# Feed-forward blocks: refilled forms, earlier weights, separate sums, and six orders of products

## The chip, the cores and the metric

The kernel runs on one core of one Trainium2 chip. The metric is the device time in microseconds (us). TensorE (PE in the profile) multiplies, VectorE (DVE) and ScalarE (ACT) work on tiles, GpSimd (POOL) does small jobs, and SyncE (SP) issues most of the DMAs, in the order of its queue. Weight loads of PE are listed as PEld.

## The reference

One layer of a decoder is computed for 1024 prompt tokens and 8 sample tokens, 1032 columns in all, in fp32:

```
x += W_merge( g_A*conv_branch + g_B*ssd_branch + g_C*mem_attn_branch )
x += SwiGLU(RMSNorm(x))          # D_MODEL 1024, FFN_HIDDEN 2816
final RMSNorm
swiglu(xn) = (silu(xn @ w_gate) * (xn @ w_up)) @ w_down
```

The mixers read one wide input projection `w_in` (12320 columns); the feed-forward part (FFN) has 22 blocks of 128 hidden rows (j = 0 to 21) each for gate and up, and then the down projection.

## The kernel before

Activations lie transposed, with 128 channels on the partitions and the 1032 tokens along the row. A product in fp32 is made from three: each operand is split into a high part `hi` (a copy rounded by ACT, `S.copy`) and a rest `lo` (`V.tensor_sub`, DVE), and PE adds hi·hi, hi·lo and lo·hi.

Most of the input projection and nearly all of the FFN go through `strassen` (L302). It takes two blocks of 128 output channels, splits weights and activations into quadrants (two halves of the contraction, two halves of 516 tokens), and needs 7 products instead of 8. `st_prod` (L254) is one product: 4 slices of the contraction (kt), 3 split terms, 2 parts of the columns (`HALF`: 256 and 260), 24 matmuls; a block has 7 products and 168 matmuls. Its order is: slice, term, part.

The seven sums of activations, the *forms* B11, T1, nT2, B21, T3, B22, T4, are made once for all blocks and kept as `hi` and `lo` tiles of the pool `ap_` (tags `ah` and `al`, 12 buffers each; T4 has a pool of its own). Two slices share one tile of 2 x 520 columns, of which 2 x 516 are used. The weights of a block come as `raw1` and `raw2` (pool `raw`, three buffers); `st_adds2` (L291) writes two sums of weights into `raw1` itself, and four `st_split` make the weight pairs A, S, T and D (three buffers for `hi`, three for `lo`). The three PSUM tiles m0, m1 and m2 change roles from block to block (L320): the tile of the last product (`pa`) is the tile of the next block's fourth (`pc`, B21).

In the FFN, `hidden_pair` runs `strassen` for gate and up of two blocks; then silu and the elementwise product (L1850 to L1852) follow on ACT and DVE. For j below 16 the forms of the product are written to DRAM (`hf_d`), for j from 16 on the product itself (`h_d`). The down projection (`d00` to `d06`, `d10` to `d16`, two halves of the contraction with four blocks each) is again `strassen`, adding into the residual rows x that are read back from DRAM (L1873). Its forms take the place of the old ones: `used(f)` is called when a block has finished with form f, and in the last block before a change (`u20` and `d06`) it calls `h_form` (L1833): two DMAs of 516 KB into tiles of the pool `ev` (5 buffers), then at once the split into the form's tiles (L389 on ACT, L390 on DVE). The last six hidden blocks go through the plain `gemm` (L204; 16 to 18) and a last stage (19 to 21).

The pool `ev` also holds the accumulators of the convolutions (`ax`, `sacc`), rows of the sampled states (`sr`), and one sum of weights (`sa`) of each FFN block.

The order of each engine's queue isn't the order of the text: Tile's planner places an instruction as soon as its inputs and its buffer are free by its own reckoning, the earlier text first. On the chip each queue then runs in that fixed order. So a load of the weights of `d00`, which stands after all of `h_form` in the text, is issued at 2203.0 us, ahead of most of the loads of the forms.

Of the kernel before, what the change touches and what calls it, by code (L numbers as in the profile page):

```python
# [17 lines left out]
P = 128  # L18
# [13 lines left out]
EPS = 1e-6  # L32
LAG = 3
GROUPS = 4
HEADS = 32
# [10 lines left out]
def tile_kernel(ctx: ExitStack, tc, a, o):  # L46
# [3 lines left out]
    def f32(t):  # L50
        return t.bitcast(F32)
# [25 lines left out]
    def pair_of(t):  # L77
        return t.rearrange("p (a c) -> p a c", a=2)[:, :, :HT]

    def act_pair(part, name):  # L80
        return pair_of(ap_.tile([P, AW], F32R, tag=part, name=name))

# [3 lines left out]
    def flat(ps):  # L86
        return banks(ps)[:, Z0 : Z0 + TT]
# [105 lines left out]

    def gemm(w, acts, name, width=P, off=0):

        hi, lo = w
        ps = mm_ps(name)
        nk = len(acts)
        n = int(pace[0] + pace[1])
        pace[1] += pace[0] - n  # L200
        marks = [nk * i // n for i in range(n)]
        between = seam.pop() if seam else None
        out = flat(ps)
        for k, (ah, al) in enumerate(acts):  # L204
# [6 lines left out]
            ks = slice(k * width + off, k * width + off + P)  # L211
            for i, (wt, x) in enumerate(((hi, ah), (hi, al), (lo, ah))):
                for c, n in FULL:
                    PE.matmul(  # L214
                        out[:, c : c + n], wt[:, ks], x[:, c : c + n],
                        start=(k == 0 and i == 0), stop=(k == nk - 1 and i == 2),
                    )
        return ps
# [6 lines left out]


    HS = [slice(0, HT), slice(HT, TT)]
    pst = [None]
# [3 lines left out]
    def hv(ps):  # L232
        return banks(ps)[:, Z0 : Z0 + HT]
# [20 lines left out]
    def st_prod(forms, ps, w, off, f, start):  # L254
        for kt in range(4):
            xh, xl = forms[f][kt]
            ks = slice(off + kt * P, off + (kt + 1) * P)
            for i, (wt, x) in enumerate(((w[0], xh), (w[0], xl), (w[1], xh))):
                for c, n in HALF:
                    PE.matmul(  # L260
                        hv(ps)[:, c : c + n], wt[:, ks], x[:, c : c + n],
                        start=(start and kt == 0 and i == 0), stop=(kt == 3 and i == 2),
                        skip_group_check=True,
                    )

# [24 lines left out]

    def st_adds2(raw1, raw2, sa):  # L291

        V.tensor_add(raw1[:, :512], raw1[:, :512], raw2[:, :512])
        V.scalar_tensor_tensor(
            raw1[:, 512:], sa[:, 512:], -1.0, raw1[:, 512:], op0=ALU.mult, op1=ALU.subtract
        )
        return raw1

    def st_sums2(raw1, raw2, sa, nm):
        return st_split(st_adds2(raw1, raw2, sa), f"{nm}T")  # L300

    def strassen(  # L302
        src1, src2, forms, nm, sums, outs, early=None, after_t3=None, ready=None, hook=None, into=False, refill=None
    ):
# [8 lines left out]
        def used(f):  # L313
            if refill is not None:
                refill(f)


        if ready is None and early is None:
            raw1, raw2 = st_raw(src1, f"{nm}r1"), st_raw(src2, f"{nm}r2")
# [8 lines left out]
        if early is None:  # L328
            pc = st_ps(tags[2], f"{nm}{tags[2]}")
            wA = st_split(raw1, f"{nm}A")  # L330
            prod(pa, wA, 0, "B11", True)
        else:
            tick()
# [11 lines left out]
        if ready is None:  # L345
            sb = st_adds2(raw1, raw2, sa)
        if early is None:
# [28 lines left out]
        tick()  # L376
        wD = st_split(raw2[:, 512:], f"{nm}D", 512)
        prod(pa, wD, 0, "T4", False)
# [1330 lines left out]
    forms = {}  # L1709
    fx = {}  # L1710

    def form(f, kt, src):
# [4 lines left out]
        split_to(*forms[f][kt], src)  # L1717

# [48 lines left out]
    pfx = st_stack.enter_context(tc.tile_pool(name="fx", bufs=2))  # L1767
    fx["T4"] = lambda part, nm: pair_of(pfx.tile([P, AW], F32R, tag=part, name=nm))

# [31 lines left out]
    g0 = (*g0, st_sums2(*g0[:3], "g0"))  # L1801
# [7 lines left out]
    def hidden_pair(nm, j, refill=None):  # L1809
# [12 lines left out]

        src = ffn[nm]
        pa = strassen(
            wblock(src, j * P), wblock(src, (j + 1) * P), forms, f"{nm}{j}",
            ev_sums, outs, e, ready=g0 if (nm, j) == ("g", 0) else None, refill=refill,
        )
        return o[0], o[1], pa if e is None else pa
# [4 lines left out]
    def h_form(ch, f):  # L1833

        for i in range(2):
            t = ev_tile(f"hf{ch}{f}{i}", (P, 2 * HT))
            SY.dma_start(t, hf_d[ch, FORMS.index(f), i])
            mk = fx.get(f) or act_pair
            hi, lo = mk("ah", f"h{ch}{f}{i}h"), mk("al", f"h{ch}{f}{i}l")
            split_to(hi, lo, t.rearrange("p (a c) -> p a c", a=2))  # L1840
            hforms[ch][f] += [(hi[:, a], lo[:, a]) for a in range(2)]

    hs = {}
    for j in range(0, NF, 2):
        s1, s2, pa = hidden_pair("g", j)
# [3 lines left out]
        u1, u2, pa = hidden_pair("u", j, (lambda f: h_form(0, f)) if j == NF - 2 else None)  # L1849
        V.tensor_mul(s1, s1, u1)  # L1850
        V.tensor_mul(s2[:, HS[1]], s2[:, HS[1]], u2[:, HS[1]])
        V.scalar_tensor_tensor(s2[:, HS[0]], pa, -1.0, s2[:, HS[0]], op0=ALU.mult, op1=ALU.mult)  # L1852
        if j >= 16:
            SY.dma_start(h_d[j - 16], s1)
            SY.dma_start(h_d[j - 15], s2)
# [10 lines left out]
    def w_rows(ch, m):  # L1866

        src = a["w_ffn_down"][0, ch * 1024 : (ch + 1) * 1024, m * P : (m + 1) * P]
        return src.rearrange("(k t p) c -> p t k c", t=2, p=P)

    for m in range(KD):
        x2[m] = big(f"x3_{m}")
        SY.dma_start(x2[m], x2_d[m])  # L1873
    for ch in range(2):
        for m in range(0, KD, 2):
            strassen(
                w_rows(ch, m), w_rows(ch, m + 1), hforms[ch], f"d{ch}{m}", ev_sums,
                lambda m=m: (x2[m][:, HS[0]], x2[m][:, HS[1]], x2[m + 1][:, HS[0]], x2[m + 1][:, HS[1]]),
                into=True, refill=(lambda f: h_form(1, f)) if ch == 0 and m == KD - 2 else None,
            )  # L1880
# [20 lines left out]
    def down(js, hs):  # L1901
        nk = len(js)
        for m in range(KD):
            nm = f"wd{js[0]}{m}"
            if nk * 256 <= 1024:
                if m % 2 == 0:
# [4 lines left out]
                    )  # L1911
                ps = gemm(w, hs, f"pd{js[0]}{m}", 256, (m % 2) * P)
            else:
# [101 lines left out]
```

## Time and profile before

| | |
|---|---|
| time, median of 3 runs | 2505.39 us (2504.51 to 2506.88) |
| the profiled execution: time, span | 2509.08 us, 2505.8 us |
| PE busy, matmuls | 2434.5 us (97%), 18906 |
| DVE, ACT, POOL busy | 1596.0, 1070.7, 116.3 us |
| mean granted clock of PE | 0.99 |
| an undisturbed block of `strassen` in the FFN, 168 matmuls | 19.93 us |
| gate and up blocks 6 to 20 | 1914.3 to 2233.1 us |
| down blocks | 2233 to 2411 us |

All times of instructions are us from the start of the span. A line "L260" is line 260 of the kernel before. In a timeline, the number in square brackets is how long the engine stood idle before the instruction, with what released it. PEclk is the granted clock of PE as a share of its full rate. The chain of waits goes from the last instruction back to what released each step.

### The profile page before, as it was taken

The numbers are of one execution on the slowest core, as the hardware profiler recorded it, in microseconds if no ns is written. First come the engines' busy times: TensorE is split into PE (matmuls) and PEld (weight loads), VectorE is DVE, ScalarE is ACT, GpSimd is POOL, SyncE is SP. The second block draws the span as 40 slices with busy tenths as digits, with TensorE's granted clock in tenths as the row PEclk, the third lists the DMA queues.
The fourth block names the chain that finished last, engine by engine and source line by source line (L and its number), as shares of the span: only waits on it lengthen the run. The fifth ranks groups of instructions, "written<-read, shape, count | busy, mean of one in ns | idle before, by whom it ended". The sixth has DMA issues, their size and how long they took to land.

```text
span 2505.8 us, 45588 instructions
## 1 busy us (share of the span) xinstructions
PE 2434.5 (97%) x18906; PEld 2315.8 (92%) x18906; DVE 1596.0 (64%) x2598; ACT 1070.7 (43%) x1716; POOL 116.3 (5%) x163
## 2 busy tenths in 40 slices
PE   7999999999999999999999989999999999999998
PEld 5899999999999999888888877899999999989998
DVE  5754586777677674656767562454777556566655
ACT  6554455354545435556544441223443333343222
POOL 0200010000000000221120000000000000000000
PEclk9999999999999999999999999999999999999999
DMA  6345434334344446567878677765444323274321
GB/s 197 106 128 167 131 107 145 114 117 127 124 127 128 134 150 209 171 214 253 265 230 283 202 262 237 263 235 158 149 158 127 110 89 111 68 268 141 100 85 68
DMA packets 356077, 404.80 MB, mean 162 GB/s; under 512 B 16422, under 2 KB 286870, under 8 KB 355863
## 3 DMA queue, kind: packets, MB, share of 16 engines
q1 hardware_dynamic: 335422, 344.18, 44.0%
q10 hardware_dynamic: 20449, 57.71, 5.9%
q8 instruction: 148, 2.42, 0.4%
q14 instruction: 58, 0.48, 0.1%
HBM read 286.74 MB, written 115.32 MB: 160 GB/s over the span
## 4 chain that ended last, share of the span: by engine, by line
PE 56%; DMA 4%; DVE 3%; ACT 1%; issue 1%; SPq 0%; ACTq 0%; DVEq 0%
PE po L214 12%; PE pm L1738 4%; PE ps_q L214 3%; PE pd L214 1%; PE py L981 1%; PE pss L994 1%; PE po L973 1%; PE d00m L260 1%; PE d10m L260 1%; PE Z14m L260 1%; PE G16m L260 1%; PE B6m L260 1%; PE C7m L260 1%; PE d16m L260 1%; PE d14m L260 1%; PE d02m L260 1%
## 5 line engine op out<-in xcount | busy, mean ns | idle before, releaser
L926 ACT ACTIVATE r<-r,acum 128x128 f32<-128x128 f32 x256 | 79.1, 391 | 3.8 <-DMA r<-ac_d 3.3
L867 ACT ACTIVATE st<-st,es 128x128 f32<-128x128 f32 x128 | 41.6, 394 | 61.4 <-DMA st<-in_state_ssm_dram 51.5
L697 DVE SCALAR_TENSOR_TENSOR ax<-u,prm,ax 128x1024 f32<-128x1024 f32 x44 | 56.3, 1280 | 0.0
L958 POOL TENSOR_TENSOR xdd<-xdt,decst 128x512 f32<-128x512 f32 x32 | 38.9, 1216 | 288.3 <-DVE xdt L954 288.3
L1385 DVE TENSOR_TENSOR yr<-po,yr 128x1032 f32<-128x1032 f32 x8 | 9.8, 1231 | 55.9 <-PE po L214 45.9
L977 DVE TENSOR_TENSOR y<-po,ea 128x512 f32<-128x512 f32 x28 | 19.3, 689 | 37.8 <-PE po L973 37.8
L952 DVE TENSOR_TENSOR r<-r,cbm 128x1024 f32<-128x1024 f32 x32 | 39.2, 1224 | 2.4
L869 DVE SCALAR_TENSOR_TENSOR st<-sr,dts,st 128x128 f32<-128x128 f32 x128 | 39.4, 345 | 0.4
L951 ACT COPY bT<-bp 128x128 f32<-128x128 f32 x32 | 8.5, 266 | 69.7 <-DVE cbm L949 69.5
L1950 ACT ACTIVATE fj<-psy 128x512 f32<-128x512 f32 (+1 forms) x18 | 10.7, 596 | 59.0 <-PE psy L1948 58.9
L981 PE MATMUL py<-r,xdt 128*64 128x128 f32 x512 | 35.0, 279 | 0.0
L873 DVE SCALAR_TENSOR_TENSOR sr<-st,sr 128x128 f32<-128x128 f32 x128 | 34.4, 285 | 0.8
L927 ACT ACTIVATE r<-r 128x1024 f32<-128x1024 f32 x32 | 33.8, 1057 | 0.6
L954 DVE TENSOR_TENSOR xdt<-xp,dtT 128x512 f32<-128x512 f32 x32 | 21.9, 684 | 19.0 <-PE xp L947 18.8
L1745 DVE TENSOR_TENSOR x<-pm,xT 128x516 f32<-128x516 f32 x16 | 11.1, 695 | 35.1 <-PE pm L1738 35.1
L994 PE MATMUL pss<-xdd,bT 128*128 128x512 f32 x64 | 33.3, 602 | 0.0
L766 ACT ACTIVATE ax<-ax 128x1032 f32<-128x1032 f32 x22 | 23.5, 1068 | 19.5 <-DVE ax L700 19.4
L981 PEld LDWEIGHTS py<-r,xdt 128*64 128x64 f32 x512 | 27.3, 136 | 4.2 <-issue 0.5
L973 PE MATMUL po<-bc,s 128*128 128x128 f32 x224 | 29.7, 275 | 1.0 <-DVE s L1000 1.0
L1007 POOL TENSOR_TENSOR s<-s,cdec 128x512 f32<-128x512 f32 x28 | 30.2, 1080 | 7.3 <-DVE s L1000 6.6
L973 PEld LDWEIGHTS po<-bc,s 128*128 128x128 f32 x224 | 27.6, 191 | 2.7 <-issue 1.6
L1667 DVE TENSOR_TENSOR gt<-po,gt 128x1032 f32<-128x1032 f32 x8 | 9.8, 1230 | 30.0 <-PE po L214 27.8
(9065 smaller groups left out, 9013.2 us busy)
## 6 DMA issues: line engine op xcount, KB each, us to landing
r<-ac_d SPq DMA_DIRECT2D x32, 512.0 KB
gt<-gt_d SPq DMA_DIRECT2D x24, 516.0 KB
xs_d<-ax ACTq DMA_DIRECT2D x22, 516.0 KB
gt_d<-G ACTq DMA_DIRECT2D x20, 516.0 KB
x<-xs_d SPq DMA_DIRECT2D x16, 516.0 KB
zs<-zs_d SPq DMA_DIRECT2D x16, 516.0 KB
yb_d<-x SPq DMA_DIRECT2D x16, 516.0 KB
in<-yb_d SPq DMA_DIRECT2D x16, 516.0 KB
```

What stands on the lines that cost most here:

```text
L214: PE.matmul(out[:, c : c + n], wt[:, ks], x[:, c : c + n], start=(k == 0 and i == 0), stop=(k == nk - 1 and i == 2),)
L260: PE.matmul(hv(ps)[:, c : c + n], wt[:, ks], x[:, c : c + n], start=(start and kt == 0 and i == 0), stop=(kt == 3 and i == 2), skip_group_ ...
L697: V.scalar_tensor_tensor(acc[:, :T], u[:, j : j + T], w[j], acc[:, :T], op0=ALU.mult, op1=ALU.add)
L867: S.activation(st[:, i], st[:, i], AF.Copy, scale=es[:, g * 4 + i, b : b + 1])
L869: V.scalar_tensor_tensor(st[:, i], rb, dts[:, g * 4 + i, b : b + 1], st[:, i], op0=ALU.mult, op1=ALU.add)
L926: S.activation(r[:, j, :], r[:, j, :], AF.Relu, scale=-1.0, bias=acum[:, c, h : h + 1])
L952: V.tensor_tensor(r, r, bc(cbm.unsqueeze(1), [P, HPG, P]), op=ALU.mult)
L958: G.tensor_tensor(b3(xdd, HPG), b3(xdt, HPG), bc(decst[:, c, hs].unsqueeze(2), [P, HPG, 64]), op=ALU.mult)
L973: PE.matmul(po[:, t * P : (t + 1) * P], state["s"][:, t * P : (t + 1) * P], bcg[1][:, cs], start=True, stop=True,)
L981: PE.matmul(py[hp : hp + 64, (h // 2) * P : (h // 2 + 1) * P], xdt[:, h * 64 : (h + 1) * 64], r[:, (h % 2) * 4 + h // 2, :], start=True, s ...
L994: PE.matmul(pss, bT, xdd, start=True, stop=True)
L1738: PE.matmul(hv(ps)[:, c : c + n], wt[:, ks], x[:, half * HT + c : half * HT + c + n], start=(k == 0 and i == 0), stop=(k == KD - 1 and i = ...
```

## The change

It has eight parts.

1. **Pads.** The 28 tiles of the FFN's forms keep their 2 x 4 unused columns and GpSimd sets them to zero (`with_pads`).
2. **Orders.** `st_prod` can run all slices and terms of one part of the columns before the next (`by_part`), can take the terms in the order hi·hi, lo·hi, hi·lo (`shared`), and can use parts of 256 and 264 columns, the pads included (`WIDE`). Six pairs of gate and up blocks (j = 8, 10, ..., 18) take six combinations; all other blocks run as before.
3. **gemm.** In the plain `gemm` of blocks 16 to 18, four of the eight products go part by part, two of them also with the other order of terms.
4. **Sums.** `st_adds2` writes its two sums into a tile of its own (`sb`, from the pool of `sa` or from `ev`) and no longer into `raw1`.
5. **Refilled forms.** `h_form` loads straight into the form's `lo` tile; the split (now in place) is issued three `used` later (`LATE`).
6. **Following weights.** In `u20` and `d06` the next block's `raw1` is loaded and split (A) within the block, and the split D stands ahead of the product T3.
7. **Last product.** The elementwise product of j = 20 moves from the end of its pair into `d00`, ahead of that block's second matrix product (`hook`).
8. **Residual rows.** Four of the eight rows x are read at the old place, the other four after the moved product.

```diff
+    def with_pads(t):
+        t = t.rearrange("p (a c) -> p a c", a=2)
+        if padded[0]:
+            G.memset(t[:, :, HT:].bitcast(F32), 0.0)
+            return t
+        return t[:, :, :HT]
...
-    def gemm(w, acts, name, width=P, off=0):
+    def gemm(w, acts, name, width=P, off=0, parts=0):
...
+        for c, n in FULL if parts else ():
+            for k in range(nk):
+                for i in range(3):
+                    product(k, i, c, n)
...
+    WIDE = ((0, 256), (256, 264))
...
     def st_prod(forms, ps, w, off, f, start):
...
+            wt, x = ((w[0], xh), (w[1], xh), (w[0], xl))[i] if shared else ((w[0], xh), (w[0], xl), (w[1], xh))[i]
...
+        if by_part:
+            for c, n in half:
+                for kt in range(4):
+                    for i in range(3):
+                        product(kt, i, c, n)
+        else:
+            for kt in range(4):
+                for i in range(3):
+                    for c, n in half:
+                        product(kt, i, c, n)
...
-        V.tensor_add(raw1[:, :512], raw1[:, :512], raw2[:, :512])
+    def st_adds2(raw1, raw2, sa, nm, sums):
+        sb = sums(f"{nm}sb")
+        V.tensor_add(sb[:, :512], raw1[:, :512], raw2[:, :512])
...
         def used(f):
-            if refill is not None:
-                refill(f)
+            turning.append(refill(f) if refill is not None else None)
+            if len(turning) > LATE:
+                g = turning.popleft()
+                if g is not None:
+                    g()
...
+        if following is not None:
+            raw = st_raw(following, f"{nm}f")
+            wD = st_split(raw2[:, 512:], f"{nm}D", 512)
         tick()
         prod(pa, wT, 0, "T3", False)
...
-        wD = st_split(raw2[:, 512:], f"{nm}D", 512)
+        if following is None:
+            wD = st_split(raw2[:, 512:], f"{nm}D", 512)
+        else:
+            ahead.append((raw, st_split(raw, f"{nm}F")))
         prod(pa, wD, 0, "T4", False)
...
+    ORDERS = {
+        8: (True, False, HALF), 10: (True, True, HALF), 12: (False, False, WIDE),
+        14: (True, True, WIDE), 16: (True, False, WIDE), 18: (False, True, HALF),
+    }
...
     def h_form(ch, f):
...
-            t = ev_tile(f"hf{ch}{f}{i}", (P, 2 * HT))
-            SY.dma_start(t, hf_d[ch, FORMS.index(f), i])
...
+        for i, (hi, lo) in enumerate(pairs):
+            SY.dma_start(f32(lo), hf_d[ch, FORMS.index(f), i].rearrange("p (a c) -> p a c", a=2))
...
+        def split():
+            for hi, lo in pairs:
+                S.copy(hi, f32(lo))
+                V.tensor_sub(lo, f32(lo), f32(hi))
...
+        if j == NF - 2:
+            continue
+        product()
...
+    residual(0, 1, 2, 3)
+
+    def opening():
+        product()
+        residual(4, 5, 6, 7)
...
-                ps = gemm(w, hs, f"pd{js[0]}{m}", 256, (m % 2) * P)
+                ps = gemm(w, hs, f"pd{js[0]}{m}", 256, (m % 2) * P, (0, 1, 2, 0)[m // 2])
```

More of the change, by code (lines that the diff above doesn't have):

```diff
@@ L203, in gemm, with product @@
         out = flat(ps)
+        def product(k, i, c, n):
+            ah, al = acts[k]
+            ks = slice(k * width + off, k * width + off + P)
+            if parts == 2:
+                wt, x = ((hi, ah), (lo, ah), (hi, al))[i]
+            else:
+                wt, x = ((hi, ah), (hi, al), (lo, ah))[i]
+            PE.matmul(
+                out[:, c : c + n], wt[:, ks], x[:, c : c + n],
+                start=(k == 0 and i == 0), stop=(k == nk - 1 and i == 2),
+            )
         for k, (ah, al) in enumerate(acts):
@@ L210, in gemm @@
                 tick()
-            ks = slice(k * width + off, k * width + off + P)
-            for i, (wt, x) in enumerate(((hi, ah), (hi, al), (lo, ah))):
+            if parts:
+                continue
+            for i in range(3):
                 for c, n in FULL:
[L214 to L217, printed above, removed]
+                    product(k, i, c, n)
+        for c, n in FULL if parts else ():
+            for k in range(nk):
+                for i in range(3):
+                    product(k, i, c, n)
         return ps
@@ L254, in st_prod, with product @@
     def st_prod(forms, ps, w, off, f, start):
-        for kt in range(4):
+        by_part, shared, half = order[0]
+        whole = banks(ps)[:, Z0 : Z0 + HT + 4]
+        def product(kt, i, c, n):
             xh, xl = forms[f][kt]
             ks = slice(off + kt * P, off + (kt + 1) * P)
[L258 to L264, printed above, removed]
+            wt, x = ((w[0], xh), (w[1], xh), (w[0], xl))[i] if shared else ((w[0], xh), (w[0], xl), (w[1], xh))[i]
+            PE.matmul(
+                whole[:, c : c + n], wt[:, ks], x[:, c : c + n],
+                start=(start and kt == 0 and i == 0), stop=(kt == 3 and i == 2),
+                skip_group_check=True,
+            )
+        if by_part:
[5 more added lines that the diff above has]
+            for kt in range(4):
+                for i in range(3):
+                    for c, n in half:
+                        product(kt, i, c, n)
     def st_early(blocks, forms):
@@ L289, in st_sums, with st_sums2 @@
         return raw1, raw2, sa, st_split(sa, f"{nm}S")
-    def st_adds2(raw1, raw2, sa):
-        V.tensor_add(raw1[:, :512], raw1[:, :512], raw2[:, :512])
+    def st_adds2(raw1, raw2, sa, nm, sums):
+        sb = sums(f"{nm}sb")
+        V.tensor_add(sb[:, :512], raw1[:, :512], raw2[:, :512])
         V.scalar_tensor_tensor(
-            raw1[:, 512:], sa[:, 512:], -1.0, raw1[:, 512:], op0=ALU.mult, op1=ALU.subtract
+            sb[:, 512:], sa[:, 512:], -1.0, raw1[:, 512:], op0=ALU.mult, op1=ALU.subtract
         )
-        return raw1
-    def st_sums2(raw1, raw2, sa, nm):
-        return st_split(st_adds2(raw1, raw2, sa), f"{nm}T")
+        return sb
+    def st_sums2(*args):
+        return st_split(st_adds2(*args), f"{args[3]}T")
+    ahead = []
+    turning = deque()
     def strassen(
-        src1, src2, forms, nm, sums, outs, early=None, after_t3=None, ready=None, hook=None, into=False, refill=None
+        src1, src2, forms, nm, sums, outs, early=None, after_t3=None, ready=None, hook=None, into=False,
+        refill=None, following=None,
     ):
@@ L313, in used @@
         def used(f):
-            if refill is not None:
-                refill(f)
-        if ready is None and early is None:
+            turning.append(refill(f) if refill is not None else None)
[3 more added lines that the diff above has]
+                    g()
+        lead = ahead.pop() if ahead else None
+        if lead is not None:
+            raw1, raw2 = lead[0], st_raw(src2, f"{nm}r2")
+        elif ready is None and early is None:
             raw1, raw2 = st_raw(src1, f"{nm}r1"), st_raw(src2, f"{nm}r2")
@@ L345, in strassen @@
         if ready is None:
-            sb = st_adds2(raw1, raw2, sa)
+            sb = st_adds2(raw1, raw2, sa, nm, sums)
         if early is None:
@@ L1716, in form @@
             forms.setdefault(f, []).extend(tuple(t[:, i, :] for t in pair) for i in range(2))
-        split_to(*forms[f][kt], src)
+        split_to(*(t[:, :HT] for t in forms[f][kt]), src)
     def form_first(kt):
@@ L1767, in tile_kernel @@
     pfx = st_stack.enter_context(tc.tile_pool(name="fx", bufs=2))
[L1768 removed]
+    fx["T4"] = lambda part, nm: with_pads(pfx.tile([P, AW], F32R, tag=part, name=nm))
     ffn = {"g": a["w_ffn_gate"][0], "u": a["w_ffn_up"][0]}
@@ L1865, in tile_kernel, with residual @@
             SY.dma_start(hf_d[j // 8, f, kt // 2][:, (kt % 2) * HT : (kt % 2 + 1) * HT], t)
[L1866 to L1873, printed above, removed]
+    def residual(*ms):
+        for m in ms:
+            x2[m] = big(f"x3_{m}")
+            SY.dma_start(x2[m], x2_d[m])
+    residual(0, 1, 2, 3)
+    def opening():
+        product()
+        residual(4, 5, 6, 7)
     for ch in range(2):
         for m in range(0, KD, 2):
+            turn = dict(refill=lambda f: h_form(1, f), following=w_rows(1, 0)) if ch == 0 and m == KD - 2 else {}
             strassen(
```

46 lines of the change are left out of this document (30 added, 16 removed).

## The prediction

> **What bounds the kernel now.** I read the page first: PE is busy nearly throughout, so only idle stretches of PE, its clock, or the time of one matmul can be won or lost.
>
> ```profile
> span 2505.8 us, 45588 instructions
> ```
>
> ```profile
> PE 2434.5 (97%) x18906; PEld 2315.8 (92%) x18906; DVE 1596.0 (64%) x2598; ACT 1070.7 (43%) x1716; POOL 116.3 (5%) x163
> ```
>
> Then the chain of waits through the stage that the change touches. A block is 168 matmuls in 19.93 us there, one after another, except at two seams, where the forms are refilled:
>
> ```profile
> 2213.20 8.32 PE u20m L260 x70
> ...
> 2229.53 5.21 DMA hf0T<-hf_d
> ...
> 2237.13 1.14 DVE g20o L1850
> 2238.28 0.60 DVE g20o L1851
> 2238.88 0.62 DVE g20o L1852
> ...
> 2239.54 22.74 PE d00m L260 x164
> 2262.28 19.93 PE d02m L260 x168
> ```
>
> ```profile
> 2302.13 1.44 PE d06m L260 x12
> ```
>
> ```profile
> 2350.67 19.93 PE d12m L260 x168
> ```
>
> From the start of u20 to the start of d02 are 2262.28 - 2213.20 = 49.08 us; two undisturbed blocks are 39.86. Seam A costs 9.22 us. From d06 to d12 are 48.54 us: seam B costs 8.68. Together **17.9 us**. The timeline of PE shows what is idle in it and for whom:
>
> ```profile
> 2239.54 0.80 PE L260 MATMUL d00m<-h0B210h,d00Ah 128*128 128x256 f32 x2 [5.94 <-DVE g20o L1852]
> ```
>
> ```profile
> 2326.02 0.50 PE L260 MATMUL d10m<-h1B210h,d10Ah 128*128 128x256 f32 x2 [3.49 <-DVE x L381]
> ```
>
> ```profile
> 2328.75 0.80 PE L260 MATMUL d10m<-h1B110h,d10Al 128*128 128x256 f32 x2 [2.00 <-DVE d10Al L248]
> ```
>
> So 5.94 and 5.49 us are idle; most of the rest is the clock, at half rate after the gap (PEclk is the third number from the end):
>
> ```profile
> 2230.00:2235.00 5.00, 3.60 (x31) 3.39 (x29) 4.86 (x5) 3.11 (x4) 0.00 (x0) 1.00 1.00 378
> ```
>
> ```profile
> 2240.00:2245.00 5.00, 5.00 (x24) 4.80 (x24) 4.34 (x6) 2.09 (x2) 0.00 (x0) 0.50 0.98 301
> ```
>
> In each case PE waits for a short DVE instruction that had long had its input: in the chain it stands behind splits (L390), and these behind loads of the forms (5.21 us of DMA), which wait for one of five `ev` tiles. DVE isn't full. In 40 us around each seam it is busy 31.30 and 32.48, 16.88 of the first with the 14 splits alone:
>
> ```profile
> 2213.00:2253.00 40.00, 34.06 (x262) 33.65 (x261) 31.30 (x33) 21.48 (x24) 0.00 (x0) 0.87 0.89 305
> 2302.00:2342.00 40.00, 34.51 (x267) 34.10 (x266) 32.48 (x36) 19.91 (x21) 0.00 (x0) 0.91 0.54 172
> ```
>
> ```profile
> 2213.00:2253.00 40.00, 16.88 (x14) 0.87 0.89 305
> ```
>
> **Parts 5 to 8: the seams.** The instructions stay (14 loads, 28 halves of splits, the product of 1.23 + 0.69 + 0.69 us at L1850 to L1852); they move. Loads no longer wait for `ev`, but for PE to be done with the form. A product takes 19.93 / 7 = 2.85 us, so B11 can load from 2216.05, and T4 from 2233.1. A load is 516 KB:
>
> ```profile
> hf0T<-hf_d SPq DMA_DIRECT2D x6, 516.0 KB
> ```
>
> 14 of them are 7.4 MB, at the 301 to 378 GB/s above 20 to 25 us, so the last lands at 2236 to 2241 if they run back to back, and a T4 issued at 2233.1 with the 5.21 us of the chain at 2238.3. The first form can be split from 2221.5. `d00` needs T4 last, when its sixth product ends: 2233.13 + 6 x 2.85 = 2250.2. DVE thus has 28.7 us for the 16.9 of the splits. The rest of its work: 31.30 - 16.88 = 14.4 us in the window, and 5.0 more, because PE now gets 9.2 us further in it and a calm stretch costs DVE 54.47 per 100:
>
> ```profile
> 2100.00:2200.00 100.00, 100.00 (x846) 100.00 (x845) 54.47 (x69) 31.46 (x41) 0.00 (x0) 1.00 0.31 98
> ```
>
> That is 0.49 us per us, 13.9 in 28.7: 30.8 us of work in 28.7, an excess of 2.1. The same for seam B gives (32.48 - 16.9 + 4.7) / 40 x 28.7 + 16.9 = 31.4, an excess of 2.7. I estimate that these 4.8 us stay as waits of PE, plus 1.2 for the four rows x, which in the trace are issued behind the last form:
>
> ```profile
> 2229.91 1.88 SPq L1873 DMA_DIRECT2D x<-x_d  x4
> ```
>
> In the changed kernel `d00` adds into x after its first product (2235.98), and PE needs that PSUM tile again at 2238.8. Issued behind T4 at 2233.1, x has 5.7 us for 3 x 516 KB, 4.2 us at 378 GB/s and a DMA's latency; DVE waits there, and behind it the splits of T3 and the moved product. The moved product must be done before `d00`'s B21 (2241.7), 2.6 us of DVE with 3 us of room. The early split of A lies in DVE's calm part. So 6.0 of 17.9 us stay: **-11.9**. Bounds: -17.9 if all is hidden; -3, if DVE's queue still stands behind loads for most of the time. No loss beyond today's, since the count of instructions is the same and the same DVE queue already waits for all 14 loads.
>
> The clock decides over part of it. C0 and C2, two blocks of the mixers, stand still for the same time, and only C0 loses its clock (0.93 over the block, against 1.00):
>
> ```profile
> 436.44 0.54 PE L260 MATMUL C0m<-xnh,C0Th 128*128 128x256 f32 x2 [2.00 <-ACT c L311]
> ```
>
> ```profile
> 580.54 0.50 PE L260 MATMUL C2m<-xnh,C2Th 128*128 128x256 f32 x2 [2.01 <-ACT c L311]
> ```
>
> ```profile
> 422.80:446.50 23.70, 21.70 (x169) 21.50 (x169) 13.73 (x33) 12.38 (x26) 1.12 (x2) 0.93 0.46 135
> 567.00:589.30 22.30, 20.29 (x170) 20.08 (x170) 13.70 (x33) 12.15 (x27) 1.23 (x2) 1.00 0.48 142
> ```
>
> 23.7 - 22.3 = 1.4 us is the price of one such loss; a half of it at one seam is within my 1.2. (The Trainium skill, "TensorE: Matmul & The Clock Gate", section "HAM oscillation — how this bites in real kernels", asks only that PE has no gaps of more than about 3.4 us. By that rule, waits of 2 to 3 us would cost no clock and the sum would be some 0.7 us better; C0's row is against it: 2.00 us were enough.)
>
> **Part 2: orders.** Before, a matmul takes 19.93 us / 168 = 118.6 ns for a mean of 258 columns. In `by_part` the matmuls of one PSUM bank follow each other, and the weights change twice as often. Such a sequence exists twice, with 256 columns:
>
> ```profile
> 184.22 0.28 PE L1248 MATMUL ps_kv<-wkv21h,memh 128*128 128x256 f32 x1
> ```
>
> ```profile
> 186.26 0.28 PE L1248 MATMUL ps_kv<-wkv21h,memh 128*128 128x256 f32 x1
> ```
>
> ```profile
> 1396.97 0.28 PE L1571 MATMUL psa<-kTh,q10h 128*128 128x256 f32 x1
> ...
> 1399.68 0.28 PE L1573 MATMUL psa<-kTh,q11l 128*128 128x256 f32 x1
> ```
>
> The first are 18 steps in 2.04 us, 113.3 ns; the second 23 steps in 2.71 us, 117.8. Scaled to 258 columns: 114.2 and 118.7. So a matmul gains 4.4 ns or nothing. I take -1.0, nearer to the second, whose stationary operand is a slice of a long tile as here. Eight blocks (j = 8, 10, 14, 16) have 1344 such matmuls: **-1.3 us**, bounds -5.9 and +0.5. The upper end is from the mixers' blocks, 0.06 us longer for the same order over other tiles, eight times:
>
> ```profile
> 877.33 19.99 PE C7m L260 x168
> ```
>
> (The Trainium skill, same page, section "Step-by-step: what each phase is for", says that loading is decoupled so that one load can serve many matmuls. By that, the old order, which keeps a weight for two parts, would save loads that `by_part` pays for. The page of the profile shows x18906 loads for x18906 matmuls, so the old order saves none; by the row nothing is lost.) `shared` changes neither columns nor loads: 0. `WIDE` adds 4 columns to 84 matmuls in each of six blocks: 504 x 4 x 118.6 / 258 ns = **+0.9 us**. **Part 3** reorders 4 x 27 matmuls: at the same prices within 0.5 us, taken as 0.
>
> **Part 1: pads.** 28 memsets on GpSimd, at 0.10 us each:
>
> ```profile
> 428.46 0.10 POOL L717 MEMSET su<- 128x2 f32 x1 [15.84 <-DMA gt_d<-G]
> ```
>
> 2.8 us on an engine that is idle in this stage (0.00 in every window above 2100), beside DVE's splits. If a split waited for each, 2.8 us; I take 0.
>
> **Part 4: sums.** The same instructions with another destination. In the FFN PE waits for no weights, so the earlier free `raw1` wins nothing. In the mixers C0, C2 and C6 stand still 2.00, 2.01 and 2.67 us:
>
> ```profile
> 867.07 0.80 PE L260 MATMUL C6m<-xnh,C6Th 128*128 128x256 f32 x2 [2.67 <-ACT c L311]
> ```
>
> ```profile
> 435.00 0.40 ACT L867 ACTIVATE st<-st,es 128x128 f32<-128x128 f32 x1 [5.05 <-DMA st<-in_state_ssm_dram]
> ```
>
> ACT's copy c stands behind work that waits 5.05 us for a sampled state. The state's load stands on SP's queue behind a load of weights that waited for `raw1`, but also behind the store of the former state; so I take 0 for part 4, with -8 us (these waits and two losses of clock gone) at one end. The other end is the third rival's.
>
> **Sum.** -11.9 - 1.3 + 0.9 = **-12.3 us**. The profiled execution took 2509.08 us (span 2505.8 and 3.3 around it) and would take 2496.8; the median of the runs lies 3.7 lower: 2505.4 - 12.3 = **2493 us**.
>
> **Rivals.** (a) The wait moves to the loads: with 7.4 MB and 2.1 MB of x in 25 us, 380 GB/s, the queue needs all that any window above moved. If at 301 GB/s x and the last forms come 6.5 us late, gain 5.4 of 17.9: 2500 us. For it: the 0.98 and 1.00 of DMA share; against it: weights and x can be placed earlier by the planner. (b) The seams go and the C blocks' waits too, or `by_part` runs at the first row's rate: 2493 - 8 - 4.6 = 2480 us. (c) Slower: `sb` needs a sixth tile where `ev` has five. In the mixers two accumulators live for three blocks, `sr` for two or more, and a sum that waits for a tile stops DVE and with it T3's weights. 40 blocks of the mixers take such a tile. It decides from (12.3 + 5) / 40 = 0.43 us for each, or five losses like C0's 2.00 + 1.4; at 0.5 us for each, 2513 us. Against it: `sb` lives only from its sums to the split of T. (d) The change doesn't do what it says: the planner places the deferred splits where it believes the loads landed, and DVE stands behind loads as before: about 2504 us.
>
> **How the numbers follow.** The forecast has 0.55, (a) 0.15, (b) 0.10, (c) 0.12, (d) 0.08. A difference below 0.2%, 5 us, can't be told from none. Faster (below 2500.4): the forecast, (b), and half of (a): 0.72. Slower (above 2510.4): (c), 0.12. The same: 0.16. The forecast's own range is 2493 - 10.6 to 2493 + 8.9 + 1.8 (seam and order bounds, the likelier inner part 2486 to 2500). For 8 in 10 I go down to (b), 2480, and up to 2507, beyond (a) and (d).
>
> **What would show it.** Seams right: u20 to d02 and d06 to d12 near 43 us each, no gap of PE above 3 us, d00's PEclk near 1. Wrong: a wait for an L390 successor or for x of 4 us or more. Orders: g8, g10 and g16 between 19.2 and 20.1 us, g12 at 20.08, g18 at 19.93; beyond 20.3, the price of an order is missing here. Sums: C0 to C6 as before; new gaps behind an `sb` show (c). The forecast falls if the sum of the seams stays above 12 us or the mixers change by more than 5.

## The result, and the profile after

The changed kernel takes **2485.34 us** (median of 4 executions, 2484.15 to 2490.69); the kernel before, run beside it, 2506.14 us. The ratio is 0.992, with a 95% interval of 0.990 to 0.994: 20.8 us faster. The time lies in the predicted range, 7.7 us below the forecast of 2493. The profiled execution took 2490.69 us, with a span of 2488.9. The first lines of its page:

```profile
span 2488.9 us, 45683 instructions
...
PE 2432.2 (98%) x18906; PEld 2313.6 (93%) x18906; DVE 1586.9 (64%) x2598; ACT 1073.0 (43%) x1716; POOL 120.7 (5%) x191
```

Line 290 is now what was line 260 (the matmul of `st_prod`), L354 to L438 the sums of a block, L924 the scaling of the sampled state (before: L867), L1906 and L1907 the split of a form. The chain of waits, with start, length and number of matmuls, first through the mixers and the hidden blocks:

```profile
423.45 19.99 PE C0m L290 x168
...
844.29 19.99 PE C6m L290 x168
...
1925.44 19.93 PE u6m L290 x168
1945.37 20.00 PE g8m L290 x168
...
1985.41 20.03 PE g10m L290 x168
...
2025.43 20.16 PE g12m L290 x168
...
2106.05 20.14 PE g16m L290 x168
...
2146.32 19.99 PE g18m L290 x168
```

C0 and C6 no longer stand still (before, from start to start, they took 23.78 and 24.67 us). The six pairs with new orders are each a little longer than the 19.93 of u6. The chain goes on through seam A and seam B:

```profile
2186.32 19.91 PE g20m L290 x168
2206.23 4.05 PE u20m L290 x34
2210.34 6.72 DMA h0T10l<-hf_d
2217.14 1.05 ACT h0T10h L1906
2218.20 0.27 ACT u20o L356
...
2271.41 19.93 PE d04m L290 x168
2291.34 17.09 PE d06m L290 x144
...
2333.41 19.93 PE d12m L290 x168
```

From g20 to d04 are 2271.41 - 2186.32 = 85.09 us. Four undisturbed blocks are 79.7, so seam A costs 5.4 us, where it cost 9.2. From d06 to d12 are 42.07 us: seam B costs 2.2, where it cost 8.7. The longest wait of PE in both is this one, in PE's timeline:

```profile
2237.66 0.51 PE L290 MATMUL d00m<-h0nT20h,d00Sh 128*128 128x256 f32 x2 [1.21 <-DVE x L354]
```

The stretches of the timeline say the same. Columns: stretch, length, busy time of PE, PEld, DVE, ACT, POOL, then PE's granted clock, DMA share and GB/s:

```profile
300.00:960.00 660.00, 658.77 (x5528) 657.78 (x5527) 483.06 (x939) 320.06 (x457) 31.79 (x78) 1.00 0.43 131
2190.00:2270.00 80.00, 76.42 (x631) 75.15 (x631) 53.39 (x64) 32.44 (x37) 0.00 (x0) 1.00 0.66 216
2270.00:2350.00 80.00, 78.49 (x658) 78.03 (x658) 59.66 (x74) 27.93 (x29) 0.00 (x0) 1.00 0.47 146
```

The clock is 1.00 in all three. In the mixers 5528 matmuls run from 300 to 960 us, where the same stretch before had 5424:

```profile
300.00:960.00 660.00, 650.49 (x5424) 648.44 (x5423) 479.69 (x932) 312.61 (x449) 29.86 (x78) 0.99 0.42 126
```

The table sorts the difference by stretches, from the starts of PE's first matmuls in the two profiled executions:

| stretch | before | after | difference |
|---|---|---|---|
| mixers, X0 to G18 | 614.8 | 602.4 | **-12.4** |
| G18 to the first product of the FFN | 833.2 | 838.4 | +5.2 |
| first products of the FFN to g8 | 163.7 | 162.7 | -1.0 |
| g8 to g20, the six pairs with new orders | 239.1 | 240.9 | **+1.8** |
| seam A, g20 to d04 | 88.9 | 85.1 | **-3.8** |
| seam B, d06 to d12 | 48.5 | 42.1 | **-6.5** |
| the rest | | | -0.3 |

The sum is -16.9, as the two spans differ (2488.9 - 2505.8). The times of the two profiled executions differ by 18.4 and the medians by 20.8, since the profiled execution of the changed kernel is 5.4 us above its median, and that of before 2.9. The +5.2 in the second stretch is no more than what executions differ by there: two kernels of the experiments, e3 and e6, run the same instructions in the same order. From G18 to g6 one needs 961.79 us and the other 954.80, on two chips; e7, on the chip of e6, needs 958.6. First e3, then e6:

```profile
942.55 20.00 PE G18m L290 x168
...
1904.34 19.93 PE g6m L290 x168
```

```profile
943.98 20.00 PE G18m L290 x168
...
1898.78 19.93 PE g6m L290 x168
```

### The profile page after: what moved, and what is told of

The parts are those of the page before. It is cut to its first block, busy times and chain, and to the rows that moved or that the text cites. A ratio compares the mean times of both kernels' runs of the same rounds, so it can differ in the third digit from the quotient of the medians.

```text
span 2488.9 us, 45683 instructions
## 1 busy us (share of the span) xinstructions
PE 2432.2 (98%) x18906; PEld 2313.6 (93%) x18906; DVE 1586.9 (64%) x2598; ACT 1073.0 (43%) x1716; POOL 120.7 (5%) x191
## 4 chain that ended last, share of the span: by engine, by line
PE 88%; DMA 5%; DVE 4%; ACT 2%; issue 1%; SPq 0%; ACTq 0%; DVEq 0%; POOL 0%
PE po L222 12%; PE pm L1796 4%; PE ps_q L222 3%; PE ps_g L222 1%; PE pd L222 1%; PE py L1038 1%; PE pss L1051 1%; PE po L1030 1%; PE Z4m L290 1%; PE g14m L290 1%; PE g12m L290 1%; PE u14m L290 1%; PE g16m L290 1%; PE u12m L290 1%; PE u16m L290 1%
## 5 line engine op out<-in xcount | busy, mean ns | idle before, releaser
L924 ACT ACTIVATE st<-st,es 128x128 f32<-128x128 f32 x128 | 41.6, 393 | 23.5 <-DMA st<-in_state_ssm_dram 23.5
L1175 DVE SCALAR_TENSOR_TENSOR x<-x,prm,sqa 128x1032 f32<-128x1032 f32 x16 | 19.7, 1289 | 14.0 <-ACT sqa L1171 14.0
```

The source lines that it names most:

```text
L924: S.activation(st[:, i], st[:, i], AF.Copy, scale=es[:, g * 4 + i, b : b + 1])
```

## The experiments

For each kernel, from its trace, in us: X0 to G18; g8 to g20; what the seams cost above undisturbed blocks; the median and the ratio to the runs of before on the same chip. Those took 2505.5 us (median) beside e1 to e4, 2507.9 beside e5 to e8, 2507.5 beside e9 to e12.

| kernel | mixers | g8 to g20 | seam A | seam B | median | ratio (95%) |
|---|---|---|---|---|---|---|
| before | 614.8 | 239.1 | 9.2 | 8.7 | 2506.1 | |
| after | 602.4 | 240.9 | 5.4 | 2.2 | 2485.3 | 0.992 (0.990 to 0.994) |
| e1, sums only | 602.5 | 239.1 | 9.7 | 8.2 | 2491.8 | 0.994 (0.993 to 0.996) |
| e2, all but the sums | 614.1 | 240.9 | 13.5 | 9.3 | 2511.9 | 1.003 (1.002 to 1.004) |
| e3, no orders, no pads | 602.5 | 239.1 | 5.6 | 2.0 | 2482.6 | 0.991 (0.988 to 0.993) |
| e4, sums, raw1 held | 606.5 | 239.1 | 17.6 | 8.3 | 2511.8 | 1.003 (1.002 to 1.004) |
| e5, state on GpSimd | 600.6 | 239.1 | 9.5 | 6.5 | 2493.2 | 0.994 (0.993 to 0.996) |
| e6, e3 with LATE = 0 | 602.3 | 239.1 | 8.3 | 5.3 | 2487.8 | 0.992 (0.991 to 0.994) |
| e7, e3 without part 6 | 602.3 | 239.1 | 3.9 | 1.9 | 2481.2 | 0.989 (0.987 to 0.991) |
| e8, e3 without 7 and 8 | 602.9 | 239.1 | 9.1 | 1.2 | 2485.9 | 0.991 (0.990 to 0.993) |
| e9, e7 with state on GpSimd | 601.4 | 239.1 | 4.2 | 1.6 | 2483.7 | 0.990 (0.989 to 0.992) |
| e10, e9 with LATE = 2 | 601.4 | 239.1 | 5.8 | 1.9 | 2484.0 | 0.990 (0.988 to 0.992) |
| e11, e7 with sums in raw1 | 614.3 | 239.1 | 13.3 | 9.0 | 2512.8 | 1.002 (1.001 to 1.003) |
| e12, e9 with LATE = 4 | 601.4 | 239.1 | 5.5 | 1.4 | 2484.7 | 0.991 (0.989 to 0.993) |

**e1 and e2: the sums alone, and all but the sums.** The edit of e1 in the kernel before (e2 takes the same lines back in the changed kernel):

```diff
-        V.tensor_add(raw1[:, :512], raw1[:, :512], raw2[:, :512])
+        sb = sums(f"{nm}sb")
+        V.tensor_add(sb[:, :512], raw1[:, :512], raw2[:, :512])
...
-            raw1[:, 512:], sa[:, 512:], -1.0, raw1[:, 512:], op0=ALU.mult, op1=ALU.subtract
+            sb[:, 512:], sa[:, 512:], -1.0, raw1[:, 512:], op0=ALU.mult, op1=ALU.subtract
```

> The kernel before with part 4 alone (the two sums of weights go into a tile of their own, sb). Theory S: the 12 us that the mixers gained from 300 to 960 us come from part 4, although I had put it at nothing. Then C0, C2, C4 and C6 are 19.99 us each (before: 23.78, 22.26, 21.75, 24.67), u0 falls from 15.55 to 14.41, both seams stay as before (49.08 and 48.54 us from u20 to d02 and from d06 to d12), and the time is 2506.1 - 12.4 - 1.1 = 2492.6 us. Rival O: the mixers gained from another part (a different order of the engines' queues that came with the rest of the change); then C0, C2, C4 and C6 stay within 0.5 us of before, and the time within 2 us of it.

> The changed kernel with part 4 undone (the sums go into raw1 again, no tile sb). Theory S: the stalls of C0, C2, C4 and C6 are back (together 12 us), u0 is back at 15.55, and the seams keep what they gained or lose little: 2485.3 + 12.4 + 1.1 = 2499 us. Rival O: C0 to C6 stay at 19.99 us, and the time is within 3 us of 2485. Rival (c) of the prediction in a weak form (sb costs tiles of ev in the FFN): the seams get faster without sb, by up to 3 us.

e1 is as theory S has it: C0, C2, C4 and C6 are 19.99 us, the mixers 12.3 us shorter, the seams within 0.5 us of before, the median 13.7 us lower. e2 brings the mixers' stalls back (24.09, 21.81, 21.50, 24.53), but it also loses the gain of both seams, which no theory expected. Parts 5 to 8 without part 4 make seam A 4.3 us longer than before, not 3.8 shorter. PE's waits in e2 from 2190 to 2290 us (total, times, longest) name the cause:

```profile
PE d00m L290 <- ACT d00Sh L275: 8.6, 1, 8.6
```

The split waits for the weights of `d00`. SP's queue in e2, and then in the changed kernel:

```profile
2204.31 0.93 SPq L267 DMA_DIRECT2D u20f<-in_w_ffn_down_dram  x2
2215.79 0.59 SPq L1900 DMA_DIRECT2D h0B110l<-hf_d  x1
...
2235.16 0.52 SPq L1900 DMA_DIRECT2D h0T41l<-hf_d  x1
2236.03 2.79 SPq L1950 DMA_DIRECT2D x<-x_d  x4
2238.92 1.23 SPq L267 DMA_DIRECT2D d00r<-in_w_ffn_down_dram  x2
```

```profile
2196.01 0.93 SPq L267 DMA_DIRECT2D u20f<-in_w_ffn_down_dram  x2
2199.82 0.92 SPq L267 DMA_DIRECT2D d00r<-in_w_ffn_down_dram  x2
2207.49 0.59 SPq L1901 DMA_DIRECT2D h0B110l<-hf_d  x1
```

With the sums in `raw1` the second weights of `d00` are placed behind 14 loads of forms and four of x; with `raw1` free early they stand ahead of all of them. Seam B is alike: in e2 PE waits 5.49 us there for the split S of `d10`.

**e4 and e5: why the mixers' stalls go.** e4 is e1 with one line more. e5 is the kernel before with the state's scaling on another engine:

```diff
             wT = st_split(sb, f"{nm}T")
+            V.tensor_copy(sb[:, 0:2], raw1[:, 0:2])
```

```diff
-            S.activation(st[:, i], st[:, i], AF.Copy, scale=es[:, g * 4 + i, b : b + 1])
+            G.tensor_scalar(st[:, i], st[:, i], es[:, g * 4 + i, b : b + 1], None, op0=ALU.mult)
```

> As the kernel before with part 4 alone, but raw1 is kept taken until the split of T, by one DVE copy of 2 columns of raw1 behind that split (the copy goes into sb, which nothing reads afterwards; 0.06 us of DVE for each block). So the sums have their own tile, but raw1 comes free as late as before. Theory S1: what the mixers gained is the earlier free raw1 (the next load of weights and the sampled state behind it on SP's queue are issued earlier); then C0, C2, C4 and C6 stand still as before, 21.7 to 24.7 us, and the time is 2506 us. Theory S2: the tile of its own is enough, because the order of ACT's queue changes with it; then they are 19.99 us, and the time is 2493 us.

> The kernel before, with one edit: the sampled state is scaled on GpSimd and no longer on ACT (128 instructions of 128x128; GpSimd is 5% busy). The sums stay in raw1. Theory Q: C0, C2, C4 and C6 stood still because of the order of ACT's queue, a scaling of the state that waits for its load ahead of the split D and the copy c that PE needs; with that instruction gone from ACT's queue they are 19.99 us each (before 23.78, 22.26, 21.75, 24.67), and the time is 2505.5 - 12 = 2493.5 us, as with part 4. Rival W: what stops them is the late load of weights on which DVE stands (C1sa, 4.3 us), or the state's own work on DVE, which now waits for a slower engine; then they stay above 21.5 us, and the time is 2505 us or more.

In e4 the four C blocks are 19.99 us although `raw1` comes free as late as before: S2. Its time misses that theory's 2493, because time is lost elsewhere (B0 and X12 take about 1 us each above an undisturbed block, g2 to g8 3.8 more than before, seam A 8.4 more). SP issues the weights of C1 at 430.45 us there and at 429.76 in the kernel before, and DVE waits 3.65 and 4.32 us for them. What differs is ACT's order. ACT in e4 (its L868 is the scaling):

```profile
433.14 0.62 ACT L247 CAST C0Dh<-C0r 128x512 fp32r<-128x512 f32 x1 [1.14 <-PE C0m L260]
433.66 0.58 ACT L311 COPY c<-C0m 128x516 f32<-128x516 f32 x1
435.85 2.16 ACT L868 ACTIVATE st<-st,es 128x128 f32<-128x128 f32 x7 [1.60 <-DVE C1sa L340]
```

In the kernel before:

```profile
435.00 0.40 ACT L867 ACTIVATE st<-st,es 128x128 f32<-128x128 f32 x1 [5.05 <-DMA st<-in_state_ssm_dram]
435.31 0.60 ACT L247 CAST C0Dh<-C0r 128x512 fp32r<-128x512 f32 x1
435.81 0.58 ACT L311 COPY c<-C0m 128x516 f32<-128x516 f32 x1
```

And in the changed kernel:

```profile
431.80 0.62 ACT L275 CAST C0Dh<-C0r 128x512 fp32r<-128x512 f32 x1 [1.14 <-PE C0m L290]
432.32 0.58 ACT L356 COPY c<-C0m 128x516 f32<-128x516 f32 x1
435.94 1.28 ACT L924 ACTIVATE st<-st,es 128x128 f32<-128x128 f32 x4 [3.04 <-DMA st<-in_state_ssm_dram]
```

The scaling that waits for the state's load starts no earlier in the changed kernel than before (12.7 us after C0's first matmul, before 12.1), but the copy c for which PE waits stands ahead of the scaling now, and behind it before. e5 shows it without any change of sums: DVE still waits 4.26 us for the weights of C1 (theory W's cause), and no C block stands still (C0, C2, C4 and C6 take 19.99 us each; the median is 2493.2 us, as theory Q has it):

```profile
430.77 0.69 DVE L340 TENSOR_TENSOR C1sa<-C1r 128x512 f32<-128x512 f32 x1 [4.26 <-DMA C1r<-in_w_in_dram]
```

```profile
561.31 19.99 PE C2m L260 x168
```

So the stall was one instruction's place in ACT's queue. (The Trainium skill, "PSUM — Partial Sum Buffer", section "Engine vs sequencer instructions", says that ScalarE's queue is strict first in, first out; the rows agree: the split D and the copy stand behind the scaling through its 5.05 us.) Why the planner turns the order when the sums have a tile of their own wasn't tried.

**e3: without orders and pads.**

```diff
-    padded[0] = True
+    padded[0] = False
...
-        8: (True, False, HALF), 10: (True, True, HALF), 12: (False, False, WIDE),
-        14: (True, True, WIDE), 16: (True, False, WIDE), 18: (False, True, HALF),
...
-                ps = gemm(w, hs, f"pd{js[0]}{m}", 256, (m % 2) * P, (0, 1, 2, 0)[m // 2])
+                ps = gemm(w, hs, f"pd{js[0]}{m}", 256, (m % 2) * P, 0)
```

> The changed kernel without parts 1, 2 and 3 (no pads, all blocks and all products of gemm in the old order). Theory P: an order has a price of its own that the blocks show (the twelve blocks together +1.83 us over 19.926 each); then they are all 19.92 to 19.94, and the time is 2485.3 - 1.8 = 2483.5 us, the seams unchanged. Rival Q: the twelve blocks are longer because of what runs beside them (GpSimd's memsets, the earlier weights), not because of their order; then they stay above 20.0, and the time at 2485. If by_part had gained at all, as I forecast (-1.3), the blocks 8, 10, 14 and 16 would now be longer than they were.

All twelve blocks are back at 19.93, the stretch is 1.8 us shorter, and so the price belongs to the orders (P) and not to what runs beside them. Nor is it the pads': in the changed kernel u6 and g20 have them too, with the old order, and take 19.93 and 19.91. From the first matmul of d12 to the last of the kernel both need 147.8 us: part 3 costs nothing. The medians differ by 2.8 us, within the intervals.

**e6 to e8: which part carries the seams.** Edits of e3: `LATE = 0`; `following=...` left out at both places; the product at the end of its pair, with all eight rows x read there.

> The kernel of the experiment without orders and pads (2482.6 us), with LATE = 0: the forms are still loaded straight into their tiles, but each is split at once, as in the kernel before. Theory L: the deferral is what lets DVE and ACT pass the loads; without it DVE stands behind the loads as before, seam A (from g20 to d04, four blocks and what they lose) goes from 85.34 towards 88.9 us and seam B (d06 to d12) from 41.8 towards 48.5: 2482.6 + 3.6 + 6.7 = 2493 us. Rival T: the loads that no longer wait for ev are enough, the planner places the splits by its own reckoning of the landing anyway; then both seams stay within 1 us and the time is 2483 us.

> The kernel of the experiment without orders and pads, without part 6: the weights of d00 and d10 are loaded and split A in their own block, and D stands behind T3 again. Theory F: with the sums in a tile of their own, three raw buffers give the next block's weights early enough without part 6; the split A then stands behind splits of forms on DVE, 1 to 3 us at each seam: 2482.6 + 4 = 2487 us. Rival G: part 6 carries most of the seams' gain, since the planner puts loads of weights that stand later in the text behind all 14 loads of forms; then PE waits 6 to 9 us for the weights of d00 and d10, as without the sums (8.63 us): 2482.6 + 12 = 2495 us.

> The kernel of the experiment without orders and pads, without parts 7 and 8: the elementwise product of j = 20 stands at the end of its pair again and all eight residual rows are read there. Theory R: the product's 2.6 us of DVE and the rows are hidden either way, the seams change by less than 1.5 us: 2482 to 2484 us. Rival M: ahead of d00 the product holds up DVE's splits of the forms and the weights for d00, 2.6 us or more at seam A, none at seam B: 2485 to 2487 us.

e6: L, with a smaller size at seam B (3.3 us for 6.7). Splitting at once gives back 2.7 of seam A and 3.3 of seam B, and the time, 2487.8 us, lies between those of the two theories. What the seams keep against before, 0.9 and 3.4 us, comes from the direct loads or from the other parts; no run takes the direct loads out alone. e7: neither. Part 6 isn't needed; without it seam A is 1.7 us shorter. The weights of `d00` are loaded ahead of the forms all the same, and PE's longest wait is one of 1.2 us for DVE's sum into x.

e8: M. Seam A loses 3.5 us, and its longest wait is in `d00`, where DVE is late with the sum into x; seam B loses nothing. Which of the two parts does it wasn't tried:

```profile
PE d00m L290 <- DVE x L354: 3.1, 1, 3.1
```

**e11: sums in raw1, without part 6.** e7 with the edit of e2.

> The kernel of the experiment without orders, pads and following weights (2481.2 us), with the sums in raw1 again. With following weights and sums in raw1, PE waited 8.63 us for the weights of d00, and seam A lost 13.5 us, seam B 9.3; with sums in their own tile 5.4 and 2.2 with following weights, 3.9 and 1.9 without. Theory B: three raw buffers are too few only when following weights take one more: the second weights of d00 had to wait behind all loads of forms for a buffer. Without part 6 the seams are then nearly as good as with the sums' own tile, 4 to 6 and 2 to 4 us lost, while C0 to C6 stand still as in the kernel before: 2481.2 + 12 + 2 = 2495 us. Theory D: it is the sums' own tile alone that lets the weights of d00 be loaded ahead of the forms; then PE waits 5 us or more for them here too, seam A loses 9 us or more: 2500 us or more.

D. PE again waits 8.6 us for the split S of `d00`, and seam A costs 13.3 us. The first weights are issued ahead of the forms (h0B110 at 2212.31 us), the second behind all of them and behind x, as SP's queue shows:

```profile
2200.88 0.94 SPq L267 DMA_DIRECT2D d00r<-in_w_ffn_down_dram  x2
...
2232.32 2.78 SPq L1948 DMA_DIRECT2D x<-x_d  x4
2235.20 2.33 SPq L267 DMA_DIRECT2D d00r<-in_w_ffn_down_dram  x2
```

So the sums' own tile decides at the seam too, with or without part 6. That it does so by the early free `raw1` is borne out by e4: there the sums have their tile and `raw1` is held, a load of `d00`'s weights is again issued behind the forms and the x (2236.66 us), and PE waits 6.50 us for the split S.

**e9, e10, e12: the useful parts together, and the size of LATE.** e9 is e7 with the edit of e5; the other two set LATE to 2 and 4 in it.

> The kernel of the last experiment but two (no orders, no pads, no following weights: 2481.2 us) with the sampled state scaled on GpSimd. It joins what the experiments found useful: the sums' own tile, forms loaded into their tiles with late splits, the moved product. Theory Q: with the sums in their own tile the order of ACT's queue is already right, so GpSimd adds only what X0 to G0 and X8 still lose (41.58 against 40.55 us, and 0.9): 2481.2 - 1.9 = 2479.3 us. Rival W: the state's work on DVE waits for GpSimd at some blocks; then 2482 us or more. In both it is faster than the kernel before (0.989).

> The kernel of the experiment sent just ahead of this one (no orders, no pads, no following weights, the sampled state on GpSimd), with LATE = 2 for 3. With LATE = 0 seam A (g20 to d04) lost 8.3 us and seam B (d06 to d12) 5.3, with 3 and following weights 5.6 and 2.0. Theory L: the wait for the load goes on growing as the split comes nearer to it: seam A 84.5 to 86, seam B 42 to 43 (LATE 3: 83.62 and 41.72), some 2 us longer in all. Rival E: the forms land 7 us after their issue and two products are 5.7 us, so that two are nearly enough, and the earlier splits take DVE out of the crowded end of the seam: both seams shorter by up to 2 us.

> As the experiment with LATE = 2, but with LATE = 4. Theory L: no wait for a load of a form is left at LATE 3 (7 us from issue to landing against three products, 8.55 us), so a fourth only moves the splits to the end, where DVE is crowded: seam A 1 to 3 us longer than 83.62, seam B 0 to 2 longer than 41.72. Rival E: at LATE 3 the splits still wait for the loads of the first forms (h0T10 was waited for); then LATE 4 is shorter by 0.5 to 1.5 us at each seam.

e9: the mixers gain 0.9 of the 1.9 us that Q expected; the median, 2483.7, would fit W, but no mixer block is longer than in e7 by more than 0.03 us, and the time can't be told from e7's. e10: at seam A theory L (5.8 for 4.2), at seam B hardly any difference. e12: L at seam A (5.5); seam B is 0.2 shorter. Over both seams three is the best of the sizes tried, by 1 us in one profiled execution of each; in the times the three can't be told apart. The shortest median of all is e7's, 2481.2 us, with parts 4, 5, 7 and 8 alone. It is below the changed kernel's, though the two intervals overlap.

## Why the prediction was right, and where it wasn't

- **Seams, -11.9 forecast, -10.3 measured.** By its own marks the step holds: u20 to d02 takes 44.4 us and d06 to d12 42.1, no wait of PE is above 1.21 us, and the clock stays at 1.00. What remains is 5.4 + 2.2 = 7.6 us, where I kept 6.0. Seam A has more left than forecast, in part by a wait of the kind that I had given to the rivals (a) and (d): ACT stands behind the split of h0T10, which waits for its load (6.72 us in the chain), and the copy u20o behind it is what PE waits 1.13 us for. Seam B has less left. But the working credited parts 5 to 8 alone. e2 shows that without part 4 they lose 4.9 us together, e11 4.4 without part 6 as well. I had checked which buffer the forms wait for, and not which one the weights of `d00` wait for. "In the FFN PE waits for no weights" held for loads in the kernel before (its 2.00 us at `d10` were for a split of weights); with parts 5 to 8 it holds only because of part 4.
- **Sums, 0 forecast, -12.4 measured in the mixers.** This is the step that failed. I had the stall and its price, and set -8 as the far end. I argued that the state's load stands behind other things too, so that an earlier free `raw1` wins nothing. The load indeed didn't get earlier; what moved was the copy c ahead of the scaling on ACT's queue. A wait has two ends, and I looked only at the one that was late. The end of -8 was too small as well: its own terms, 2.00 + 2.01 + 2.67 and two losses of 1.4, add up to 9.5; it left out C4 (1.8 us); and C0 and C6 lost 1.8 and 2.0 us beyond their waits, not 1.4 each. The four blocks together lost 12.5 us.
- **Orders, -0.4 forecast with WIDE, +1.8 measured.** No mark of 20.3 us was passed, but g12 shows 20.16 for 20.08, g16 20.14 for at most 20.1, and `by_part` costs 0.09 us a block (g8, u8, g10, u10: 20.00 to 20.03) where I forecast a gain of 0.16. The rows that I scaled from were short runs over other tiles. Their upper bound, +0.06 a block from the mixers, was the nearer one. `shared`, forecast at nothing, costs 0.07.
- **Pads and part 3 at nothing:** right (e3).
- **Rivals.** Half of (b) came about: the C blocks' waits went, `by_part` gained nothing. (c) didn't: the mixers got faster with the sixth tile; X0 to X2 alone lost 1.0 us. Where the tiles are really short it does decide: in e4 the held `raw1` makes seam A 8.4 us longer. (a) and (d) are in the 5.4 us that seam A still costs.
- **The sum.** -10.3 - 12.4 + 1.8 = -20.9, against -20.8 of the medians. That they agree so closely is partly luck, since the stretch from G18 to the FFN varies by more between executions. The forecast's own test, mixers that change by more than 5 us, says the reasons weren't complete, though the time lay in the range: the seams and the orders alone would have given 2506.1 - 10.3 + 1.8 = 2497.6 us, and the rest came from a term put at nothing.

## What to carry to other kernels

Where PE waits for a copy that stands behind another wait on its engine's queue, look at the order of that queue and not only at the late load: another tile for a sum can turn the order and free PE, and so can moving the waiting instruction to an idle engine. Before loads are allowed to start earlier, ask which other loads they will now stand ahead of, and whether those have a free buffer by then. An edit that costs time without another may pay with it (parts 5 to 8 with part 4 here), so undo each one from the whole as well as trying it alone.

## What the runs showed of the hardware

- Four more columns cost more than their share: the blocks with 264 columns and the old order are 0.22 us longer (20.16 and 20.14 against 19.93) for 84 widened matmuls, 2.6 ns each or 0.65 ns a column, where a matmul of 258 columns takes 118.6 ns, 0.46 a column.
- A gap's length doesn't decide alone whether PE loses its clock. C0 and C2 of the kernel before stand still for 2.00 and 2.01 us, and only C0 loses it. The traces show why. The granted clock is 1.00 or 0.50, and in all 14 traces it changes only at the marks of a fixed grid of 3.413 us (within 0.005 us), so that each loss but the last, which the end of the profile cuts, lasts a whole number of steps. C0's gap lies in one step; C2's is cut by a mark, with 1.6 us ahead of it. The steps with the gaps and the steps behind them, first C0, then C2:

```profile
433.36:436.77 3.41, 1.41 (x12) 1.21 (x11) 2.21 (x4) 1.77 (x5) 0.00 (x0) 1.00 0.50 125
436.77:440.19 3.42, 3.42 (x18) 3.42 (x17) 1.24 (x2) 2.62 (x7) 0.00 (x0) 0.50 0.61 153
```

```profile
576.72:580.14 3.42, 1.81 (x16) 1.60 (x14) 1.49 (x3) 1.05 (x3) 0.00 (x0) 1.00 0.70 187
580.14:583.55 3.41, 3.01 (x25) 3.01 (x26) 1.23 (x3) 3.34 (x9) 0.00 (x0) 1.00 0.42 101
```

So a loss of one step costs 1.7 us, half of it. e6's two seams hold one such step each, and e3's none. In e3 PE stood idle for 2.09 us ahead of d02, cut by the mark at 2246.49, and kept its clock. In e7 it stood for 1.35 us and soon after for 0.53, both in one step, and lost it:

```profile
2247.96 0.50 PE L290 MATMUL d02m<-h0B110h,d02Ah 128*128 128x256 f32 x2 [2.09 <-ACT d02Ah L275]
```

```profile
2246.49:2249.90 3.41, 1.89 (x13) 1.69 (x14) 2.07 (x4) 1.04 (x1) 0.00 (x0) 1.00 0.53 143
2249.90:2253.30 3.40, 3.40 (x30) 3.34 (x29) 3.16 (x5) 2.00 (x2) 0.00 (x0) 1.00 0.09 25
```

```profile
1589.65:1593.06 3.41, 1.53 (x9) 0.89 (x8) 1.52 (x2) 2.19 (x3) 0.00 (x0) 1.00 0.89 329
1593.06:1596.47 3.41, 3.41 (x13) 3.02 (x13) 3.41 (x4) 0.98 (x2) 0.00 (x0) 0.50 0.62 186
```

Of the 9040 steps at full clock between 200 and 2420 us of the 14 traces, all 42 in which PE is idle for 1.85 us or more are followed by a step at half clock; of the 8996 with 1.65 or less only five are, each at 1137 to 1150 us and with 18 matmuls of a single column among its 26 or 27; of the two between (1.77 and 1.82) one is. (The Trainium skill, "TensorE: Matmul & The Clock Gate", section "What's actually happening", says that activity is watched over a free-running window of about 3.4 us.) The grid agrees with it.
